# Eight first sums in turns by two k-tiles, the bias table in split products, and the last cross head's scores inside the output product

## The chip, the cores and the metric

One core of a Trainium2 chip runs the whole program. The metric is the device time in microseconds of one execution.

## The reference

One decoder layer on x (256 tokens, width 1024), all in float32:

```python
x = x + 0.5 * swiglu(rms_norm(x, g_ffn1), w_ffn1_gu, w_ffn1_down)   # width 2816
q/k/v = rms_norm(x, g_mix) @ w_in          # 12 dilated heads, 4 block-sparse heads
x = x + concat(rms_norm(oa), rms_norm(ob)) @ w_out    # both with a relative-position bias table
x = x + cross_attention(rms_norm(x, g_cross), rms_norm(mem, g_mem))  # 4 heads of 256, 256 memory tokens
x = x + 0.5 * swiglu(rms_norm(x, g_ffn2), w_ffn2_gu, w_ffn2_down)
out = rms_norm(x, g_final)

def swiglu(x, w_gu, w_down):
    g, u = split(x @ w_gu, 2)              # gate columns 0..2815, up columns 2816..5631
    return (silu(g) * u) @ w_down
```

The bias table is `rel_bias` (32 buckets x 16 heads), picked by a fixed one-hot matrix of buckets for 383 distances.

## The kernel before, in words

**Split products.** Weights and activations are kept as two parts in the type `float32r`, a high part (a rounded copy, written by ScalarE) and a low part (the rest, written by VectorE). A product is the sum of high x high, high x low and low x high. `wsplit` (L124) splits a weight tile, `split` (L314) an activation, with the norm's gain folded in. Activations are stored transposed, a k-tile being 128 features x 256 tokens with the high part in columns 0 to 255 and the low part in 256 to 511 of one slot. Some products are therefore one of 512 columns (high weight against both parts) and one of 256 (low weight): `mmT_run` (L219). `mmT_wide` (L232) and `mm3` (L187) do three of 256 columns.

**Weights.** A load brings 512 KB (two k-tiles x 512 columns) into one of four `raw` tiles; after the two parts of the split a raw tile is free again. The split tiles `w` are eight. All weight loads go through the SP queue. In `gate_up` (L415) each chunk takes 512 gate columns and 512 up columns (four blocks of 128 each); `each` (L262) goes block by block through all eight k-tiles of a chunk, in runs of two k-tiles.

**Order.** `start` (L754) is written out by hand for all engines (`manual_schedule()`): each engine does what the text gives it, in that order. From `gate_up` on only TensorE's order is as written, the other engines being ordered by a scheduler. Small steps are put into TensorE's stream by an estimated clock: `tick` adds the estimated time of each product, `later(delay, f)` runs f when that clock has gone on by delay, and `until` runs the waiting steps at once when a result is needed.

**The start.** x arrives in three loads and is turned by TensorE (`prepare`, L773, transposes at L779), copied to `X` and split. `prepare(j)` serves k-tiles 2j and 2j + 1 and, in the kernel before, also splits gate weight tile j. After WARM products on an identity matrix (L770, L796) come the gate sums: for each k-tile twelve products (L798), four blocks in four banks of the accumulator memory, with `prepare` of the next pair after every second k-tile. The up weights are then split, and the up sums follow (two blocks k-tile by k-tile at L811, two blocks one after the other at L816). The norm of x is applied afterwards: `token_squares` (L333) sums squares on ScalarE, `st.given` (L386) makes the root and a diagonal on GpSimd and VectorE, and `_rows` (L379) spreads it to all partitions as R by TensorE (L382). `turn_gains` (L74) transposes the other gains.

**The bias table.** `bias_table` (L88) loads a table of logarithms, the one-hot rows and `rel_bias`; `bias_rows` (L96) multiplies the last two in plain float32 (L98), adds, and sends the rows through device memory to the tables F that the attention adds to its scores. It is a hook after the second chunk of the first `gate_up`.

**Cross attention.** `cross_qp` (L678) makes the query blocks (L717), splits each, and puts `scores` of a head (L682: twelve products, then a softmax over both token halves) and its `turn` (L705: four transposes and a split) into the stream by `later`. `cross_o` (L729) multiplies the turned probabilities with V; `addT` (L466) does the output product with a written order of steps (L860), a step being (k, blocks) for k-tiles k and k + 1.

## Time and profile before

| | us |
|---|---|
| median of 3 runs (lowest, highest) | 605.53 (605.5, 606.17) |
| the profiled execution | 605.74 |
| its span | 604.0 |

The profile is of one execution. The span runs from the first to the last instruction; the rest of the time lies around it. Engines are TensorE (PE, its weight loads PEld), VectorE (DVE), ScalarE (ACT), GpSimd (POOL) and the queue SP. TensorE is busy 595.4 us of the span, VectorE 428.5, ScalarE 347.7. A row's duration on TensorE covers an instruction's own pipeline, so that neighbours overlap; the distance between starts is what an instruction costs.

### The profile page before, as it was taken

Reading aid. Unit: us, or ns where it says so; the run is one execution under the profiler, and the core shown is the slowest. Engines: PE = TensorE matmul, PEld = TensorE weight load, DVE = VectorE, ACT = ScalarE, POOL = GpSimd, SP = SyncE. Lnnn points to the kernel's source line nnn. Section 1 sums busy time; section 2 is a strip of 40 time slices with the busy share of each in tenths; the row PEclk is TensorE's granted clock in tenths of the full one; section 3 lists DMA queues with packets and bytes.
Section 4 is the critical chain, followed back from the end, with each engine's and each line's share of the span. In section 5 each row is a group of like instructions: output and inputs, shape, how many; then the busy total and the mean of one; then the engine's idle time right before and its main releaser. Section 6 shows DMA issues by size and latency. Waiting matters only on the chain.

```text
span 604.0 us, 9469 instructions
## 1 busy us (share of the span) xinstructions
PE 595.4 (99%) x3516; PEld 519.3 (86%) x3516; DVE 428.5 (71%) x716; ACT 347.7 (58%) x604; POOL 51.8 (9%) x83
## 2 busy tenths in 40 slices
PE   9999999999999999999999999999999999999995
PEld 8988888888899888888888899888888888888884
DVE  4788766887565876766897787869877877874412
ACT  6756446655554677656675565657755656653302
POOL 0000110000010102113300120003100000000000
PEclk9999999999999999999999999999999999999999
DMA  7867998677467636454446645444565565565401
GB/s 237 282 206 229 211 246 252 196 227 245 171 221 231 210 106 210 142 173 140 141 121 218 195 143 162 140 140 130 158 230 181 169 217 171 189 231 196 152 0 69
DMA packets 58989, 110.02 MB, mean 182 GB/s; under 512 B 3760, under 2 KB 14608, under 8 KB 58944
## 3 DMA queue, kind: packets, MB, share of 16 engines
q1 hardware_dynamic: 57664, 105.49, 54.1%
q0 software_dynamic: 832, 2.88, 2.8%
q10 hardware_dynamic: 448, 1.05, 0.5%
q8 instruction: 27, 0.44, 0.3%
q14 instruction: 18, 0.15, 0.1%
HBM read 107.58 MB, written 1.84 MB: 181 GB/s over the span
## 4 chain that ended last, share of the span: by engine, by line
PE 96%; issue 1%; DVE 1%; ACT 1%; POOL 0%; POOLq 0%; ACTq 0%
PE bank L224 43%; PE bank L228 22%; PE bank L188 7%; PE bank L189 7%; PE bank L190 7%; PE bank L238 5%; PE bank L518 1%; PE bank L575 1%; PE bank L558 1%; DVE w L126 0%; PE bank L770 0%; PE bank L382 0%; PE bank L779 0%; PE bank L873 0%; PE bank L604 0%
## 5 line engine op out<-in xcount | busy, mean ns | idle before, releaser
L224 PE MATMUL bank<-slot,w 128*128 128x512 f32 x1130 | 353.4, 396 | 0.0
L126 DVE TENSOR_TENSOR w<-raw,w 128x1024 fp32r<-128x1024 f32 (+1 forms) x197 | 237.3, 1219 | 84.5 <-ACT w L125 83.7
L125 ACT ACTIVATE w<-raw 128x1024 fp32r<-128x1024 f32 (+1 forms) x197 | 202.4, 1051 | 86.3 <-PE bank L190 43.4
L228 PEld LDWEIGHTS bank<-slot,w 128*128 128x128 f32 x1130 | 209.8, 188 | 48.7 <-issue 1.0
L228 PE MATMUL bank<-slot,w 128*128 128x256 f32 x1130 | 222.5, 279 | 0.0
L224 PEld LDWEIGHTS bank<-slot,w 128*128 128x128 f32 x1130 | 173.8, 189 | 2.5 <-issue 0.6
L188 PE MATMUL bank<-w,slot 128*128 128x512 f32 x152 | 60.0, 395 | 0.0
L190 PE MATMUL bank<-w,slot 128*128 128x512 f32 x152 | 59.3, 390 | 0.0
L189 PE MATMUL bank<-w,slot 128*128 128x512 f32 x152 | 59.2, 390 | 0.0
L277 ACT ACTIVATE hv<-bank 128x256 f32<-128x256 f32 x108 | 39.8, 375 | 33.7 <-PE bank L228 33.0
L320 ACT ACTIVATE slot<-u 128x512 fp32r<-128x512 f32 x22 | 13.8, 628 | 36.0 <-DVE u L434 36.0
L190 PEld LDWEIGHTS bank<-w,slot 128*128 128x128 f32 x152 | 28.5, 188 | 6.1
L188 PEld LDWEIGHTS bank<-w,slot 128*128 128x128 f32 x152 | 28.5, 188 | 6.0 <-issue 0.3
L189 PEld LDWEIGHTS bank<-w,slot 128*128 128x128 f32 x152 | 28.6, 188 | 5.5
L238 PE MATMUL bank<-slot,w 128*128 128x256 f32 x240 | 31.8, 290 | 0.0
L238 PEld LDWEIGHTS bank<-slot,w 128*128 128x128 f32 x240 | 30.1, 195 | 0.5 <-DVE slot L324 0.2
L355 POOL TENSOR_TENSOR ssq<-ssq,sq 128x256 f32<-128x256 f32 x22 | 20.5, 933 | 78.5 <-ACT sq L350 78.4
L429 ACT ACTIVATE g<-g 128x512 f32<-128x512 f32 x22 | 13.8, 631 | 20.1 <-DVE g L292 20.1
L324 DVE SCALAR_TENSOR_TENSOR slot<-X,gT,slot 128x256 fp32r<-128x256 f32 x30 | 19.4, 659 | 6.9 <-ACT slot L323 6.9
L321 DVE TENSOR_TENSOR slot<-u,slot 128x512 fp32r<-128x512 f32 x22 | 15.2, 691 | 10.7 <-ACT slot L320 10.5
L278 DVE TENSOR_TENSOR g<-bank,hv 128x256 f32<-128x256 f32 x40 | 16.5, 420 | 8.5 <-ACT hv L277 8.5
L323 ACT ACTIVATE slot<-X,gT 128x256 fp32r<-128x256 f32 x30 | 14.8, 506 | 13.0 <-DVE X L303 13.0
(128 smaller groups left out, 488.4 us busy)
## 6 DMA issues: line engine op xcount, KB each, us to landing
raw<-in_w_ffn_gu_dram SPq DMA_DIRECT2D x88, 512.0 KB, 4.6
raw<-in_w_ffn_down_dram SPq DMA_DIRECT2D x44, 512.0 KB, 4.3
raw<-in_w_ckv_dram SPq DMA_DIRECT2D x16, 512.0 KB, 5.5
raw<-in_w_in_dram SPq DMA_DIRECT2D x12, 512.0 KB, 3.7
raw<-in_w_in_dram SPq DMA_DIRECT2D x24, 256.0 KB, 4.0
raw<-in_w_out_dram SPq DMA_DIRECT2D x8, 512.0 KB, 4.5
raw<-in_w_cq_dram SPq DMA_DIRECT2D x8, 512.0 KB, 4.8
raw<-in_w_co_dram SPq DMA_DIRECT2D x8, 512.0 KB, 3.7
```

The source lines that it names most:

```text
L125: nc.scalar.activation(w[:, 0, a:b], raw[:, a:b], AF.Copy)
L126: nc.vector.tensor_tensor(w[:, 1, a:b], raw[:, a:b], w[:, 0, a:b].bitcast(F32), OP.subtract)
L188: nc.tensor.matmul(ps, ah, bh, start=start, stop=False)
L189: nc.tensor.matmul(ps, al, bh, start=False, stop=False)
L190: nc.tensor.matmul(ps, ah, bl, start=False, stop=stop)
L224: nc.tensor.matmul(ps, w[:, 0, o + blk * P:o + (blk + 1) * P], both(xs, k), start=k == first, stop=False)
L228: nc.tensor.matmul(ps[:, :256], w[:, 1, o + blk * P:o + (blk + 1) * P], both(xs, k)[:, :256], start=False, stop=k == last)
L238: nc.tensor.matmul(ps, w[:, wp_, o + blk * P:o + (blk + 1) * P], a, start=start and i == 0, stop=stop and i == 2)
L277: nc.scalar.activation(t, ps[:, 256:], AF.Copy)
L278: nc.vector.tensor_tensor(out, ps[:, :256], t, OP.add)
L324: nc.vector.scalar_tensor_tensor(l, src, g, h.bitcast(F32), OP.mult, OP.subtract)
L355: (eng or nc.gpsimd).tensor_tensor(new, self.ss, sq, OP.add)
```

## The change

In `start`, gate and up tiles are loaded, split and used in turns: for each pair of k-tiles 24 gate products (`products(j, pg0, ...)`) and 24 up products (`products(j, pu0, ...)`). A gate block and its up block share a bank, gate in columns 0 to 255 and up in 256 to 511; only the gate's first product carries the start flag. `prepare` no longer splits weights; `fetch` loads a raw tile. The first tile's first high half is written half by ScalarE and half by VectorE, and there are two products fewer in the second warm-up (an identity product is two instructions). R and the gains come with other delays.

In the bias table, `rel_bias` is split into two parts and the one-hot rows are copied to the split type, so that L98 becomes two products of 384 columns. Both are loaded into a raw tile.

In the cross attention, head 3's `scores` and `turn` are no longer put in by `later`; they are steps of the output product's order.

```diff
@@ -76,7 +76,6 @@
         nc.tensor.transpose(gps[:, :48], grow, ident[:48, :48])
         nc.vector.tensor_copy(gT, gps[:, :48])
 
-    rbt = const.tile([32, 16], F32, name="rbt")
     F = []
     X = [const.tile([P, 256], F32, name=f"X{k}") for k in range(KT)]
 
@@ -87,15 +86,22 @@
 
     def bias_table():
         lnt = work.tile([16, NB], F32, tag="g1", name="lnt", bufs=3)
-        oht = work.tile([32, NB], F32, tag="g1", name="oht", bufs=3)
         nc.sync.dma_start(lnt, lnc)
-        nc.sync.dma_start(oht, onehot)
-        nc.sync.dma_start(rbt, rel_bias)
-        later(4.0, bias_rows, lnt, oht)
-
-    def bias_rows(lnt, oht):
+        raw = rawp.tile([P, 1024], F32, tag="raw", name="raw")
+        nc.vector.memset(raw[:32, NB:384], 0.0)
+        nc.sync.dma_start(raw[:32, :NB], onehot)
+        nc.sync.dma_start(raw[:32, 512:528], rel_bias)
+        ohr = work.tile([32, 384], F32R, tag="pt", name="ohr", bufs=4)
+        rbs = small.tile([32, 2, 16], F32R, tag="rbs", name="rbs", bufs=1)
+        nc.scalar.activation(ohr, raw[:32, 0:384], AF.Copy)
+        nc.scalar.activation(rbs[:, 0], raw[:32, 512:528], AF.Copy)
+        nc.vector.tensor_tensor(rbs[:, 1], raw[:32, 512:528], rbs[:, 0].bitcast(F32), OP.subtract)
+        later(8.0, bias_rows, lnt, ohr, rbs)
+
+    def bias_rows(lnt, ohr, rbs):
         ps = bank()
-        nc.tensor.matmul(ps[:16, :NB], rbt, oht, start=True, stop=True)
+        for i in range(2):
+            nc.tensor.matmul(ps[:16, :384], rbs[:, i], ohr, start=i == 0, stop=i == 1)
         rb = work.tile([16, 384], F32, tag="u1", name="rb")
         nc.vector.tensor_add(rb[:, :NB], ps[:16, :NB], lnt)
         nc.vector.memset(rb[:, NB:], 0.0)
@@ -236,7 +242,7 @@
         for i, (wp_, a) in enumerate(((0, h), (0, l), (1, h))):
             for blk, ps in enumerate(pieces):
                 nc.tensor.matmul(ps, w[:, wp_, o + blk * P:o + (blk + 1) * P], a,
-                                 start=start and i == 0, stop=stop and i == 2)
+                                 start=start and i == 0, stop=stop and i == 2, skip_group_check=True)
                 tick(0.11)
 
     def projT(wk, xs, nblk, spread=False, whole=0, abreast=False):
@@ -700,7 +706,8 @@
                 nc.vector.reciprocal(rl, l)
                 nc.vector.tensor_scalar(pt, pt, rl, None, OP.mult)
                 pts[h][tb] = pt
-            later(5.0, turn, h)
+            if h < 3:
+                later(5.0, turn, h)
 
         def turn(h):
             tp = bank()
@@ -722,9 +729,9 @@
                     halves(t, ps)
                     ps = t
                 split(Q[-1], blk % 2, 1, ps)
-                if blk % 2:
+                if blk % 2 and (c, blk) != (1, 3):
                     later(3.0 + 3.0 * (blk // 2) * (c == 0), scores, c * 2 + blk // 2)
-        return PT
+        return PT, lambda: scores(3), lambda: turn(3)
 
     def cross_o(V, PT, OT, h):
         until(lambda: PT[h] is not None)
@@ -743,23 +750,25 @@
 
     st = Stats()
     xs = [slot() for _ in range(4)]
-    raws = [rawp.tile([P, 1024], F32, tag="raw", name="raw") for _ in range(4)]
-    ws = [wp.tile([P, 2, 1024], F32R, tag="w", name="w") for _ in range(4)]
-    first = [(ws[k // 2], (k % 2) * 512) for k in range(KT)]
-    pg0 = [bank()[:, :256] for _ in range(4)]
-
-    def load_w0(i):
-        nc.sync.dma_start(raws[i].rearrange("p (a n) -> p a n", n=512), cols(w_gu1, i * 2, 2, 0, 512))
+    gate, up = [], []
+    b0 = [bank() for _ in range(4)]
+    pg0, pu0 = [b[:, :256] for b in b0], [b[:, 256:] for b in b0]
+
+    def fetch(wk, c0):
+
+        raw = rawp.tile([P, 1024], F32, tag="raw", name="raw")
+        nc.sync.dma_start(raw.rearrange("p (a n) -> p a n", n=512), cols(w_gu1, len(wk), 2, c0, 512))
+        w = wp.tile([P, 2, 1024], F32R, tag="w", name="w")
+        wk += [(w, 0), (w, 512)]
+        return w, raw
 
     def start():
         load_x(0, 256)
         nc.scalar.dma_start(grow[0:8], g_ffn1.rearrange("l (k p) -> (l k) p", p=P))
-        load_w0(0)
+        g0, u0 = fetch(gate, 0), fetch(up, FF)
         load_x(256, 256)
-        load_w0(1)
+        g1, u1 = fetch(gate, 0), fetch(up, FF)
         load_x(512, 512)
-        load_w0(2)
-        load_w0(3)
         load_gains()
         make_identity(nc, ident)
         nc.vector.memset(ones, 1.0)
@@ -770,55 +779,71 @@
             nc.tensor.matmul(gps[:, :P], ident, ident, start=True, stop=True)
         nc.tensor.transpose(gps[:, :8], grow[0:8], ident[:8, :8])
         nc.vector.tensor_copy(gT1, gps[:, :8])
-        def prepare(j):
+        def turned(j):
             banks = [bank(), bank()] if j == 0 else [bank()] * 2
             xp = [banks[i][:, i * 256:i * 256 + 256] for i in range(2)]
             for i in range(2):
                 for tb in range(2):
                     o = tb * 512 + ((j * 2 + i) % 4) * P
                     nc.tensor.transpose(xp[i][:, tb * P:(tb + 1) * P], x0[j // 2][:, o:o + P], ident)
-            if j > 0:
-                wsplit(ws[j], raws[j], 0, 1024)
-                for i in range(2):
-                    nc.scalar.activation(X[j * 2 + i], xp[i], AF.Copy)
+            return xp
+
+        def prepare(j):
+            xp = turned(j)
             for i in range(2):
-                split(xs[j], i, 1, X[j * 2 + i] if j else xp[i], gain("ffn1", j * 2 + i))
-                if j == 0:
-                    wsplit(ws[j], raws[j], i * 512, i * 512 + 512)
-            if j == 0:
-                for i in range(2):
-                    nc.scalar.activation(X[i], xp[i], AF.Copy)
+                nc.scalar.activation(X[j * 2 + i], xp[i], AF.Copy)
+            for i in range(2):
+                split(xs[j], i, 1, X[j * 2 + i], gain("ffn1", j * 2 + i))
+
+        def products(j, pieces, wk, first):
+            for k in (j * 2, j * 2 + 1):
+                mmT_wide(pieces, wk, xs, k, first and k == 0, k == KT - 1)
 
         xss = [small.tile([P, 2], F32, tag=f"xss{hf}", name="xss", bufs=1) for hf in range(2)]
 
-        prepare(0)
-        for i in range(WARM - 1):
+        xp = turned(0)
+        split(xs[0], 0, 1, xp[0], gain("ffn1", 0))
+        w, raw = g0
+        nc.scalar.activation(w[:, 0, 0:256], raw[:, 0:256], AF.Copy)
+        nc.vector.tensor_copy(w[:, 0, 256:512], raw[:, 256:512])
+        nc.vector.tensor_tensor(w[:, 1, 0:512], raw[:, 0:512], w[:, 0, 0:512].bitcast(F32), OP.subtract)
+        split(xs[0], 1, 1, xp[1], gain("ffn1", 1))
+        wsplit(w, raw, 512, 1024)
+        wsplit(*u0, 0, 1024)
+        for i in range(2):
+            nc.scalar.activation(X[i], xp[i], AF.Copy)
+        for i in range(WARM - 2):
             nc.tensor.matmul(gps[:, :P], ident, ident, start=True, stop=True)
-        for k in range(KT):
-            mmT_wide(pg0, first, xs, k, k == 0, k == KT - 1)
-            if k % 2 == 0 and k < KT - 2:
-                prepare(k // 2 + 1)
-                if k == 2:
-                    token_squares(x0[0], xss[0])
-            if k == 5:
-                up.extend(colchunk(w_gu1, FF, 512))
-                token_squares(x0[1], xss[1])
-                nc.vector.tensor_tensor(xss[0], xss[0], xss[1], OP.add)
-                st.given(xss[0], 7.0)
-                later(4.0, turn_gains)
-        pu = [bank()[:, :256] for _ in range(2)]
-        for k in range(KT):
-            mmT_wide(pu, up, xs, k, k == 0, k == KT - 1)
-        b = bank()
-        for blk in range(2, 4):
-            pu.append(b[:, (blk - 2) * 256:(blk - 1) * 256])
-            for k in range(KT):
-                mmT(pu[-1], up, xs, k, blk, k == 0, k == KT - 1)
-        return pu
-
-    up = []
+        products(0, pg0, gate, True)
+        prepare(1)
+        wsplit(*g1, 0, 512)
+        wsplit(*g1, 512, 1024)
+        g2 = fetch(gate, 0)
+        products(0, pu0, up, False)
+        wsplit(*u1, 0, 1024)
+        u2 = fetch(up, FF)
+        products(1, pg0, gate, False)
+        prepare(2)
+        products(1, pu0, up, False)
+        wsplit(*g2, 0, 1024)
+        g3 = fetch(gate, 0)
+        token_squares(x0[0], xss[0])
+        products(2, pg0, gate, False)
+        prepare(3)
+        wsplit(*u2, 0, 1024)
+        u3 = fetch(up, FF)
+        products(2, pu0, up, False)
+        wsplit(*g3, 0, 1024)
+        token_squares(x0[1], xss[1])
+        nc.vector.tensor_tensor(xss[0], xss[0], xss[1], OP.add)
+        st.given(xss[0], 5.8)
+        later(2.0, turn_gains)
+        products(3, pg0, gate, False)
+        wsplit(*u3, 0, 1024)
+        products(3, pu0, up, False)
+
     with tc.manual_schedule():
-        pu0 = start()
+        start()
     with tc.manual_schedule(engines={mybir.EngineType.PE}):
         hid = gate_up(w_gu1, xs, st, (None, bias_table), (pg0, pu0))
         xs, st, block = next_x("mix")
@@ -851,14 +876,14 @@
         xs, st, block = next_x("cross")
         addT(w_out, ot, block)
         st.done(rows=False)
-        PT = cross_qp(xs, K, st)
+        PT, scores3, turn3 = cross_qp(xs, K, st)
         OT = []
         cross_o(V, PT, OT, 0)
         cross_o(V, PT, OT, 1)
         xs, st, block = next_x("ffn2")
         every = range(4)
-        addT(w_co, OT, block, ((0, every), (2, (0, 1)), lambda: cross_o(V, PT, OT, 2), (2, (2, 3)),
-                               lambda: cross_o(V, PT, OT, 3), (4, every), (6, every)))
+        addT(w_co, OT, block, ((0, (0, 1)), scores3, (0, (2, 3)), (2, (0, 1)), lambda: cross_o(V, PT, OT, 2), turn3,
+                               (2, (2, 3)), (4, (0,)), lambda: cross_o(V, PT, OT, 3), (4, (1, 2, 3)), (6, every)))
         st.done()
 
         hid = gate_up(w_gu2, xs, st, scale=0.5)
```

## Rows read from the trace of the kernel before

**Rows 1.** The page: the busy time of TensorE (us, share of the span, instructions), the granted clock in 40 slices, and the chain that ended last by engine.

```profile
PE 595.4 (99%) x3516; PEld 519.3 (86%) x3516; DVE 428.5 (71%) x716; ACT 347.7 (58%) x604; POOL 51.8 (9%) x83
...
PEclk9999999999999999999999999999999999999999
...
PE 96%; issue 1%; DVE 1%; ACT 1%; POOL 0%; POOLq 0%; ACTq 0%
```

**Rows 2.** The chain of waits in order of time, first 35 us: start us, us, what. L779 are the transposes of x, L796 and L770 the warm-up, L238 the products of `mmT_wide`.

```profile
1.35 2.50 PE bank L770 x10
...
4.05 1.04 PE bank L779 x4
5.09 1.71 PE bank L796 x8
...
8.75 0.44 PE bank L779 x4
9.19 3.06 PE bank L238 x24
...
12.69 2.88 PE bank L238 x24
...
16.01 6.26 PE bank L238 x49
...
22.46 3.44 PE bank L238 x27
```

**Rows 3.** The timeline of the first 40 us, all engines, around the first product: start us, us, engine, line, operation, out<-in, [idle before <-releaser].

```profile
5.62 0.63 ACT L125 ACTIVATE w<-raw 128x512 fp32r<-128x512 f32 x1 [0.44 <-DMA raw<-in_w_ffn_gu_dram]
...
6.45 2.30 PE L238 MATMUL bank<-slot,w 128*128 128x256 f32 x12
...
7.03 0.76 ACT L790 ACTIVATE X<-bank 128x256 f32<-128x256 f32 x2
```

**Rows 4.** The same timeline, around `prepare(2)`.

```profile
12.09 0.60 PE L779 MATMUL bank<-ident,slot 128*128 128x128 f32 x4
...
12.45 3.13 PE L238 MATMUL bank<-slot,w 128*128 128x256 f32 x24
...
12.73 0.66 ACT L783 ACTIVATE X<-bank 128x256 f32<-128x256 f32 x2 [0.69 <-PE bank L779]
...
14.07 0.63 ACT L337 ACTIVATE junk<-slot 128x512 bf16<-128x512 f32 x1
```

**Rows 5.** Timelines of the SP queue, ScalarE and VectorE from 10.9 to 31 us, in order of start. Of SP a row is an issue (or several merged).

```profile
10.97 0.32 SPq L93 DMA_DIRECT2D rbt<-in_rel_bias_dram  x1
...
12.48 26.43 SPq L118 DMA_DIRECT2D raw<-in_w_ffn_gu_dram  x13
...
22.04 1.06 ACT L125 ACTIVATE w<-raw 128x1024 fp32r<-128x1024 f32 x1 [1.51 <-DMA raw<-in_w_ffn_gu_dram]
...
23.00 0.61 ACT L337 ACTIVATE junk<-slot 128x512 bf16<-128x512 f32 x1
...
24.38 0.37 SPq L118 DMA_DIRECT2D raw<-in_w_ffn_gu_dram  x1
...
28.67 1.42 DVE L292 TENSOR_TENSOR g<-bank,R 128x256 f32<-128x256 f32 x4
...
29.28 1.06 ACT L125 ACTIVATE w<-raw 128x1024 fp32r<-128x1024 f32 x1 [0.99 <-DMA raw<-in_w_ffn_gu_dram]
...
30.66 1.22 DVE L126 TENSOR_TENSOR w<-raw,w 128x1024 fp32r<-128x1024 f32 x1
```

**Rows 6.** The chain of waits in order of time around the bias table's product (L98).

```profile
60.08 0.74 PE bank L98 x2
60.82 0.43 PE bank L224
61.25 0.23 PE bank L228 x2
61.49 0.47 PE bank L224 x2
```

**Rows 7.** Timelines of TensorE and VectorE around the scores of cross head 3, in order of start: L188 to L190 are the products of `mm3`, L321 on VectorE low halves (`slot<-hq` of a query block, `slot<-bank` of an output tile or of turned probabilities), L224 at 386.27 the first output product, L701 the last step of a softmax.

```profile
383.00 0.69 DVE L321 TENSOR_TENSOR slot<-bank,slot 128x512 fp32r<-128x512 f32 x1
...
383.67 0.28 PE L188 MATMUL bank<-slot 128*128 128x256 f32 x1
...
384.27 0.38 PE L188 MATMUL bank<-slot 128*128 128x256 f32 x1
...
384.74 0.42 DVE L321 TENSOR_TENSOR slot<-hq,slot 128x256 fp32r<-128x256 f32 x1
...
385.21 0.39 PE L189 MATMUL bank<-slot 128*128 128x256 f32 x1 [0.56 <-DVE slot L321]
...
386.27 0.63 PE L224 MATMUL bank<-slot,w 128*128 128x512 f32 x2
...
389.36 0.35 DVE L701 TENSOR_SCALAR cpt<-cpt,crl 128x256 f32<-128x256 f32 x1
```

**Rows 8.** Stretches of the end (from:to us, length), busy time and instructions of each engine, then PEclk (granted clock as a share of full), DMA share, GB/s.

```profile
597.60:601.70 4.10, 0.00 (x0) 0.00 (x0) 0.91 (x2) 1.39 (x3) 0.55 (x1) 1.00 0.24 90
...
601.90:604.00 2.10, 0.00 (x0) 0.00 (x0) 0.00 (x0) 0.00 (x0) 0.00 (x0) 0.50 0.12 41
```

## The prediction

> **What bounds the kernel now.** I read the page first: TensorE is busy 99% of the span, at the full granted clock in every slice, and the chain that ended last is 96% TensorE [rows 1]. The reader is to see that nothing off TensorE counts by itself; the time is the list of TensorE's instructions plus the few places where it stands still. So I next read the chain in order of time and looked for those places.
>
> At the start [rows 2] the chain is TensorE alone from 1.35 us. A group of 24 products of 256 columns takes 2.88 us where nothing waits, 0.120 us each. The groups of 24, 49 and 27 that took 3.06, 6.26 and 3.44 us therefore hold 0.18 + 0.38 + 0.20 = 0.76 us beyond that, of which I put 0.2 on the small transposes that cut into the stream: some **0.55 us of waits** is all that these groups have to give. In the bias table the two passes of L98 take 0.74 us and the product behind them 0.43 in place of 0.23 [rows 6]. In the cross attention the twelve score products of head 3 take 383.67 to 386.27, 2.60 us, against 12 x 0.120 = 1.44 us: TensorE waits first for ScalarE's high half of the last query block, then for VectorE's low half [rows 7], 1.16 us.
>
> The reference for the sum is the profiled execution, 605.74 us with a span of 604.0; the median of the runs shown is 605.53, 0.21 less. About 0.2% (1.2 us) is what a measurement of this kernel tells from no change.
>
> **First products.** The first weight tile's high half is now written half by ScalarE and half by VectorE. Before, ScalarE's 512 columns ran from 5.62 for 0.63 us and TensorE began at 6.45 [rows 3]; 256 columns take about 0.38 (the X copies' size [rows 3]), so the tile is ready 0.25 us earlier, and two fewer warm-up instructions (1.71 us for eight, 0.21 each [rows 2]) let TensorE be there. TensorE is at its lower clock level at that time (four transposes 1.04 us at 4.05, 0.44 us at 8.75 [rows 2]), so of the 0.25 I take 0.1 to 0.15. Using each x tile for gate and up halves the speed at which x and its splits are wanted, so the 0.55 us of waits should go; the diagonal for R is asked for only after all 192 products, so a wait for it can't cut in either. The order keeps as many products and transposes as before. Together **-0.7 us** (0 to -0.9; 0 if new small waits take their places, since the low half of g2 is ready about when it is wanted).
>
> **A wait that the new order makes.** All engines follow the written order in `start`. Third up pair, in the diff: `products(2, pg0)`, `prepare(3)`, `wsplit(*u2)`, `products(2, pu0)`. On ScalarE u2's split thus stands behind prepare(3), whose X copies wait for transposes that TensorE makes only after the gate products, while the very next products want u2. For the other pairs the split stands ahead of the next transposes, or a whole up group of 2.88 us lies between; here nothing does. Its length comes from prepare(2) of before, where ScalarE also waited for the transposes [rows 4]: transposes at 12.09, first X copy at 12.73, two copies and two gain splits, the next ScalarE instruction at 14.07, 1.98 us after. Then 1.06 us for u2's high half [rows 5], and 0.1 to 0.2 from ScalarE's end to a product (6.25 to 6.45 with the warm-up still ahead [rows 3]): 3.2 us after the transposes began. TensorE itself is free 0.36 us after (12.09 to 12.45 [rows 4]). Stall: **2.8 us**. The low half on VectorE ends 1.22 us after the high [rows 5], and the third group of four products wants it 8 x 0.12 = 0.96 us after the first: another 0.2 to 0.3. Behind the waiting X copies stand on ScalarE both gain splits, u2, g3, and the squares for R; all of them slide by as much, but g3 is wanted 2.9 us after u2 and follows 0.95 us behind it. I take **+3.0 us** (2.7 to 3.3). No work covers it: TensorE has nothing else in its order.
>
> Is the written order really ScalarE's? At 22.04 ScalarE stood 1.51 us for a load with the token squares behind it [rows 5], whose input the transposes of 12.09 had already read [rows 4]. That is the order as written, kept where it hurts.
>
> **The second chunk's gate weights.** Four raw tiles serve all loads. The raw tile of u3 is freed only when its low half is done. That instruction now stands on VectorE behind the copy of the gains (`turn_gains`), which waits for TensorE in the middle of the last gate group, some 2.3 us into it. Counted from the third transposes (T): TensorE resumes at T+3.2, ends the up group at T+6.3, gains turned at T+8.6, copied at T+9.1, u3's low half at T+10.4, last product and R at T+13.0. If the fourth gate tile of the second chunk takes u3's raw tile, it is loaded and its split begins 4.9 us after the issue (24.38 to 29.28 in the row of before [rows 5]): T+15.3, high half T+16.4, low T+17.6. The first block of the second chunk wants its last two k-tiles three runs of 0.70 us [rows 6] after T+13.0, T+15.1. That is a wait of 1.3 to 2.0 us, and 2.9 if the eight sums, now all read after R (0.36 us each [rows 5]), go ahead on VectorE. If another raw tile comes free earlier it is zero: loads of a later block can slip in front of `start`'s, as the bias load did at 10.97 ahead of the up loads [rows 5], so the first two splits may do so as well. I take **+0.9** (0 to 2.9), nearer to zero because of that row.
>
> **Bias table.** The two passes of 383 columns become two products of 384 in the split type. Nothing in the trace has 32 rows in that type; the nearest is L224, 512 columns in 0.23 us [rows 6], so 384 cost 0.175 and the pair 0.35 in place of 0.74. The cost at the edges (0.2 behind) I leave. **-0.4 us** (0 if the price per column stays, as the number of passes does, which also excludes a loss here; -0.6 if the edge goes too). The load of the table leaves the SP queue at 10.97 and comes, with the one-hot rows, through a raw tile: one of four is away for a load and a ScalarE copy, some 5 us, and SP's weight loads queue behind it. Eight split tiles, each worth four runs of 0.70 us (0.47 + 0.23 [rows 6]) to TensorE, cover that, and the product is planned 4 us later; without that cover one tile's 2.8 us would show. The table's result is first used in the attention, a whole half-step later. Zero.
>
> **Cross head 3.** Its twelve products move behind two runs of the output product (2 x 0.70 = 1.39 us), from 383.67 to 385.06; the fourth wants the last low half at 385.42, and VectorE had it at 385.16 [rows 7]. The first runs want the first output tile, low half done at 383.69 [rows 7]. So the 1.16 us go, up to 0.1. Late next is the softmax: before, its last step ended 389.71, 3.44 us after the scores [rows 7]; now it starts at 386.5 and its turn stands at 390.7, 0.75 us later than needed. Behind the turn, the first block of k-tiles 4 and 5 wants the third output tile 1.8 us after its product, against 0.6 + 0.7 us of splits with one weight split of 1.2 us possibly between. **-1.0 us** (-0.3 to -1.2). No DMA is issued by what moves.
>
> **Sum.** -0.7 + 3.0 + 0.9 - 0.4 - 1.0 = **+1.8 us**: 607.5 for the profiled execution, 607.3 for the median. With all ends: -0.9 + 2.7 + 0 - 0.6 - 1.2 = 0.0 to 0 + 3.3 + 2.9 + 0 - 0.3 = +5.9.
>
> **Rivals.**
> *The wait for u2 is not there (faster).* If u2's split reaches ScalarE ahead of the third prepare, TensorE runs on; the second chunk's loads then hurt by 0.3 at most: -0.7 + 0.3 - 0.4 - 1.0 = -1.8, **603.7**. For it: the early bias load on SP shows that the queues aren't wholly as written. Against it: that load belongs to no ordered block, u2's split does, and ScalarE kept its order in every row of [rows 4, 5]. It decides if the split moves up by 2 us. Chance 0.15.
> *Paid back (no change).* The stall is there, but raw tiles come free in time and bias and cross give their full ends: -0.8 + 3.0 + 0 - 0.5 - 1.1 = +0.6, **606.1**. Chance 0.25.
> *The clock falls in the stall (slower yet).* The granted clock stood at 1.00 until 601.7 and was 0.50 afterwards, the lower of the two levels; TensorE had done nothing since 597.6 [rows 8]. A stop of 2.8 us in which it issues nothing could do this amid the start. At the lower level it worked from 1.35 us into the products that begin at 6.45 [rows 3], and no longer at 8.75 [rows 2], 5 to 7.4 us at half speed; half of as long a stretch again is about 3 us: +1.8 + 3 = +4.8, **610.3**. Against it: there TensorE had stopped for good, here it goes on. Chance 0.08.
> The Trainium skill, "TensorE: Matmul & The Clock Gate", section "Why this matters for your kernels", warns of idle gaps between bursts of matmuls, after which the clock is at its lower rate; by that rule the time would be this rival's.
> The forecast itself has 0.52.
>
> **Numbers.** 607.3 us; the range 604.0 to 609.8 takes in nearly all of the forecast's own ends and the second rival, half of the first, and leaves the clock's case out. Faster by over 0.2%: 0.15 and the forecast's low end, 0.17. Same: 0.25. Slower: 0.58.
>
> **What would show it.** In the profile after: TensorE idle for 2.5 to 3 us near 23 to 26 us, released by ScalarE's split of w, with the transposes just ahead; ScalarE idle 2.5 us before those X copies; a first L224 at 35 to 36 us where it was 33.2, and a wait within 3 us behind it; L98's successors 0.35 us for two; no wait in head 3's scores. It is wrong if the 24 products behind the third transposes follow at once, or if the time falls below 605.

## The result, and the profile after

After: **612.65 us** median (612.12 to 613.49, 4 runs); before: 605.51 (605.14 to 606.17, 4 runs); ratio 1.0117 [1.0103, 1.013]. The change costs 7.1 us where 1.8 were forecast, outside the range. The profiled execution of after is 612.12 us with a span of 610.3, 6.3 longer than the span of before.

The page of after: busy time of TensorE and the others, granted clock, chain that ended last.

```profile
PE 597.0 (98%) x3514; PEld 520.6 (85%) x3514; DVE 429.1 (70%) x720; ACT 347.3 (57%) x607; POOL 52.0 (9%) x83
...
PEclk9899998999999999999999999999999999999998
...
PE 86%; DMA 6%; DVE 4%; issue 2%; ACT 2%; POOL 0%; POOLq 0%; ACTq 0%; SPq 0%; DVEq 0%
```

Against [rows 1] TensorE is busy 1.6 us longer, the clock has two new dents (slices 2 and 7, near 25 and 100 us), and the chain, 96% TensorE before, runs through DMA for 6% of the span. Something waits for loads now.

**The first stop**, timeline of TensorE from 18 to 37 us, then ScalarE's (start us, us, engine, line, operation, out<-in, [idle before <-releaser]). L788 are the transposes of x (L779 before), L244 is `mmT_wide` (L238), L230 and L234 are the two products of `mmT_run` (L224, L228 before), L131 and L132 the two halves of a split (L125, L126).

```profile
21.46 0.60 PE L788 MATMUL bank<-ident,slot 128*128 128x128 f32 x4
24.55 7.21 PE L244 MATMUL bank<-slot,w 128*128 128x256 f32 x43 [2.48 <-ACT w L131]
...
35.81 0.71 PE L230 MATMUL bank<-slot,w 128*128 128x512 f32 x2
```

```profile
22.10 0.66 ACT L794 ACTIVATE X<-bank 128x256 f32<-128x256 f32 x2 [2.75 <-PE bank L788]
...
23.44 2.00 ACT L131 ACTIVATE w<-raw 128x1024 fp32r<-128x1024 f32 x2
```

This is the forecast wait, with its two marks: the four transposes just ahead, ScalarE idle 2.75 us before its X copies. The rows of the second prepare of before [rows 4] had TensorE go on 0.36 us after the transposes; here it is 3.09. The second chunk starts at 35.81, 2.6 us later than before. Stretches of the same kernel (from:to us, length, busy time and instructions of each engine, then PEclk) show what followed both stops:

```profile
26.20:29.60 3.40, 3.40 (x18) 3.40 (x18) 2.43 (x6) 2.48 (x5) 0.72 (x1) 0.50 0.72 217
29.60:33.00 3.40, 3.40 (x28) 3.21 (x28) 1.23 (x3) 2.00 (x2) 0.00 (x0) 1.00 0.73 220
...
97.90:101.20 3.30, 2.96 (x10) 2.57 (x11) 2.90 (x6) 0.91 (x2) 0.00 (x0) 0.50 0.90 315
```

After each stop, when TensorE is already at work again, the granted clock is 0.50, the lower level (1.2 GHz), for some 3.4 us: 18 products in 3.4 us where the next 3.4 hold 28.

**The second stop** was not forecast. Timeline of TensorE, then the chain of waits in order of time (start us, us, what):

```profile
96.98 0.73 PE L230 MATMUL bank<-slot,w 128*128 128x512 f32 x2 [2.45 <-ACT w L131]
98.24 0.80 PE L234 MATMUL bank<-slot,w 128*128 128x256 f32 x2 [0.53 <-DVE w L132]
```

```profile
69.25 11.11 DMA raw<-in_w_ffn_gu_dram
...
80.38 1.07 ACT w L131
...
81.47 1.23 DVE w L132
...
82.73 13.12 DMA raw<-in_w_ffn_gu_dram
...
95.88 1.06 ACT w L131
```

Read it upwards: TensorE waits at 94.5 us for the last up tile of the fourth chunk; that tile's load took 13.12 us and could go out only when the low half of the tile before it in the same raw tile was done (82.70); and that tile's load had taken 11.11 us. Two slow loads in series use up all the slack that the split tiles hold. What is in their way, DMA traffic by queue in 72 to 76 us and in 84 to 88 us (packets, MB, share of 16 engines):

```profile
q0 software_dynamic: 87, 0.40, 97.2%
q1 hardware_dynamic: 6, 0.01, 0.8%
...
q0 software_dynamic: 239, 0.79, 98.6%
q1 hardware_dynamic: 23, 0.03, 4.6%
```

q1 carries the weights. In both stretches a weight load of the chain is under way, and q0 takes the engines: it is the bias table, its rows written 32 times and read back into F. The timeline of GpSimd's queue has it, in after and (second fence) in before:

```profile
68.40 0.84 POOL L109 DMA_DIRECT2D scr<-rb  x1 [40.43 <-DVE rb L106]
79.04 4.65 POOL L180 DMA_DIRECT2D F<-scr  x8 [9.80 <-DMA scr<-rb]
```

```profile
62.66 0.84 POOL L103 DMA_DIRECT2D scr<-rb  x1 [37.14 <-DVE rb L100]
73.71 4.63 POOL L174 DMA_DIRECT2D F<-scr  x8 [10.21 <-DMA scr<-rb]
```

The same transfers were there before, and a load of weights then also took long (the same tile's split began at 85.14 after 4.94 us of ScalarE waiting for its DMA), but it was issued at 72.99 us, not 82.73, and TensorE needed it near 92. Why the loads were late, ScalarE from 54 to 62 us of after (L96 and L97 the copies of the one-hot row and of the relative bias, L326 a hidden tile's high half):

```profile
54.75 0.20 ACT L97 ACTIVATE rbs<-raw 32x16 fp32r<-32x16 f32 x1
...
58.01 0.63 ACT L326 ACTIVATE slot<-u 128x512 fp32r<-128x512 f32 x1 [1.95 <-DVE raw L91]
58.55 0.51 ACT L96 ACTIVATE ohr<-raw 32x384 fp32r<-32x384 f32 x1
...
61.26 0.63 ACT L326 ACTIVATE slot<-u 128x512 fp32r<-128x512 f32 x1 [1.94 <-DVE u L440]
61.80 1.04 ACT L131 ACTIVATE w<-raw 128x1024 fp32r<-128x1024 f32 x1
```

The third chunk's up splits begin at 61.80; before, they began at 54.64. Ahead of them ScalarE now has both copies and two hidden tiles (L326), where before had one (53.84). The copies are short, 0.20 and 0.51 us, and L96 follows L326 without a wait. What costs is ScalarE's idling before the two hidden tiles, 1.95 and 1.94 us. The first of these rows names the memset L91, which ended at 57.98 us; the tile's own input, which VectorE makes at L440, ended at 57.97. The chain of waits in the same stretch runs through L440 both times and through neither copy (0.04 us of the bias difference, L98, stand between the first two rows):

```profile
57.38 0.60 DVE u L440
...
58.01 0.64 ACT slot L326
...
60.54 0.70 DVE u L440
...
61.80 1.05 ACT w L131
```

The tile that is split at 61.80 was asked for at 53.76 and had landed at 57.15.

**The small parts.** The bias product (timeline, first row) gives its place up after 0.44 us, in place of 0.74 [rows 6]. Head 3's twelve scores, now amid the output product, take 392.44 to 393.88, 1.44 us, the time of twelve products and no wait, where [rows 7] had 2.60.

```profile
66.54 0.52 PE L104 MATMUL bank<-ohr,rbs 32*16 32x384 f32 x2
66.98 0.39 PE L234 MATMUL bank<-slot,w 128*128 128x256 f32 x1
...
392.44 0.28 PE L194 MATMUL bank<-slot 128*128 128x256 f32 x1
...
393.88 0.63 PE L230 MATMUL bank<-slot,w 128*128 128x512 f32 x2
```

Matching L224 with L230 product by product, the shift against before is +2.60 us at 33 us, +2.40 behind the bias product, +7.29 from 101 us on, and +6.33 at the end, 0.96 having come back in head 3. So the second stop and what follows it cost 4.9 us: 2.6 for the stop, and 2.3 more because the products from 96.98 to 101.36 us take 4.38 us in place of 2.09. Of these some 0.8 are the wait for the tile's low half (98.24) and some 1.5 the lower clock.

### The profile page after: what moved, and what is told of

It is laid out like the page before. It is cut to its first block, busy times and chain, and to the rows that moved or that the text cites. A ratio compares the mean times of both kernels' runs of the same rounds, so it can differ in the third digit from the quotient of the medians.

```text
span 610.3 us, 9464 instructions
## 1 busy us (share of the span) xinstructions
PE 597.0 (98%) x3514; PEld 520.6 (85%) x3514; DVE 429.1 (70%) x720; ACT 347.3 (57%) x607; POOL 52.0 (9%) x83
## 3 DMA queue, kind: packets, MB, share of 16 engines
q1 hardware_dynamic: 57664, 105.49, 53.0%
q0 software_dynamic: 832, 2.88, 2.7%
## 4 chain that ended last, share of the span: by engine, by line
PE 86%; DMA 6%; DVE 4%; issue 2%; ACT 2%; POOL 0%; POOLq 0%; ACTq 0%; SPq 0%; DVEq 0%
PE bank L230 37%; PE bank L234 19%; PE bank L194 7%; PE bank L196 7%; PE bank L195 7%; DMA raw<-in_w_ffn_gu_dram 6%; PE bank L244 5%; DVE w L132 2%; PE bank L524 1%; PE bank L581 1%; PE bank L564 1%; ACT w L131 1%; DVE u L440 0%; PE bank L779 0%; PE bank L788 0%
## 5 line engine op out<-in xcount | busy, mean ns | idle before, releaser
L230 PE MATMUL bank<-slot,w 128*128 128x512 f32 x1130 | 354.3, 397 | 2.4 <-ACT w L131 2.4
L132 DVE TENSOR_TENSOR w<-raw,w 128x1024 fp32r<-128x1024 f32 (+1 forms) x197 | 236.5, 1216 | 82.7 <-ACT w L131 81.4
L131 ACT ACTIVATE w<-raw 128x1024 fp32r<-128x1024 f32 (+1 forms) x197 | 201.9, 1049 | 95.1 <-PE bank L196 42.8
L234 PEld LDWEIGHTS bank<-slot,w 128*128 128x128 f32 x1130 | 210.4, 189 | 50.1 <-issue 1.3
L234 PE MATMUL bank<-slot,w 128*128 128x256 f32 x1130 | 223.6, 280 | 0.5 <-DVE w L132 0.5
L230 PEld LDWEIGHTS bank<-slot,w 128*128 128x128 f32 x1130 | 174.4, 189 | 4.6 <-ACT w L131 2.6
L244 PE MATMUL bank<-slot,w 128*128 128x256 f32 x288 | 38.1, 293 | 2.5 <-ACT w L131 2.5
L244 PEld LDWEIGHTS bank<-slot,w 128*128 128x128 f32 x288 | 36.5, 199 | 3.2 <-ACT w L131 2.7
L326 ACT ACTIVATE slot<-u 128x512 fp32r<-128x512 f32 x22 | 13.8, 629 | 33.6 <-DVE u L440 31.7
L330 DVE SCALAR_TENSOR_TENSOR slot<-X,gT,slot 128x256 fp32r<-128x256 f32 x30 | 19.4, 659 | 14.2 <-ACT slot L329 14.2
L284 DVE TENSOR_TENSOR u<-bank,hv 128x256 f32<-128x256 f32 x40 | 16.7, 420 | 7.1 <-ACT hv L283 6.9
```

The lines of the kernel that those rows point to most:

```text
L131: nc.scalar.activation(w[:, 0, a:b], raw[:, a:b], AF.Copy)
L132: nc.vector.tensor_tensor(w[:, 1, a:b], raw[:, a:b], w[:, 0, a:b].bitcast(F32), OP.subtract)
L230: nc.tensor.matmul(ps, w[:, 0, o + blk * P:o + (blk + 1) * P], both(xs, k), start=k == first, stop=False)
L234: nc.tensor.matmul(ps[:, :256], w[:, 1, o + blk * P:o + (blk + 1) * P], both(xs, k)[:, :256], start=False, stop=k == last)
L244: nc.tensor.matmul(ps, w[:, wp_, o + blk * P:o + (blk + 1) * P], a, start=start and i == 0, stop=stop and i == 2, skip_group_check=True)
L284: nc.vector.tensor_tensor(out, ps[:, :256], t, OP.add)
```

## The experiments

All against the kernel before on the same chip (its medians: 605.75, 605.39 and 605.41 us in the three sets). A theory named by letters in the quoted texts is the one that the same text tells. The first set asks which part makes the stop at 94 us: the start, the bias part, both together, or the wait for u2.

**One part alone (three runs, and two together).** The edits are the hunks of the change, applied to the kernel before.

```
e1: cross_qp hands back scores(3), turn(3); addT(w_co, ...) calls them   (nothing else)
e2: fetch, turned, prepare, products and the new order in start          (nothing else)
e3: bias_table through a raw tile, two fp32r products, later(8.0, ...)   (nothing else)
e9: e1 and e3
```

> The kernel before with the cross part alone. All theories: 0.8 to 1.2 us faster than before, no wait in the scores of head 3; if the part is worth nothing by itself, within 0.3 us.

604.91 us (604.53 to 605.25, 10 runs), ratio 0.9986 [0.9977, 0.9996]: -0.84.

> The kernel before with the start part alone. The first product of the second chunk (33.2 us before) at about 35.8 us, a stop of 2.8 us near 22 us and a stretch at the lower clock behind it. Theory S (the weight loads that the start makes late are what starves TensorE at 94 us): the stop near 94 us is there too, 6 to 8 us slower in all. Theory B (the bias table's new place and raw tile starve it): no stop near 94 us, 2.3 to 3 us slower. Theory SB (it takes both): also 2.3 to 3 us.

608.61 us (608.42 to 610.55, 4 runs), ratio 1.0054 [1.0036, 1.0071]: +2.86. The profiled execution, 610.55 us, is the slowest of the four. No stop at 94 us. Another small wait shows, TensorE ahead of the bias product (its one-hot row, issued at 58.94, lands at 62.84), and in the profiled execution the lower clock comes after that wait and not after the first:

```profile
62.94 0.80 PE L98 MATMUL bank<-oht,rbt 32*16 32x383 f32 x2 [1.29 <-issue]
```

```profile
26.00:29.50 3.50, 3.45 (x30) 3.33 (x28) 2.52 (x7) 2.92 (x6) 0.72 (x1) 1.00 0.57 172
...
64.80:68.00 3.20, 3.20 (x12) 2.81 (x11) 3.17 (x7) 0.90 (x2) 0.84 (x1) 0.50 0.87 277
```

> The kernel before with the bias table's part alone. Theory S: 0.2 to 0.4 us faster, no stop. Theory B: a stop of several us near 91 us, 3 to 5 us slower. Theory SB: within 0.5 us of before, the weight tiles of the fourth chunk's up half ready later than before but in time.

605.15 us (604.81 to 605.66, 10 runs), ratio 0.9989 [0.9979, 0.9998]: -0.60. No stop at 94 us. The same copies stand on ScalarE, but only one hidden tile ahead of the third chunk's up splits:

```profile
53.73 0.63 ACT L326 ACTIVATE slot<-u 128x512 fp32r<-128x512 f32 x1 [1.94 <-DVE u L440]
...
54.53 2.00 ACT L131 ACTIVATE w<-raw 128x1024 fp32r<-128x1024 f32 x2
```

> The kernel before with the change's cross-attention and bias parts, its start as it was. If the parts add up where the start is not changed, the time is 605.4 less 0.8 and 0.6, 603.8 to 604.4 us, with no wait over 0.3 us between 80 and 100 us; if the bias part, with its raw tile, already costs the weight loads something that the cross part does not hide, 604.8 us or more.

604.19 us (603.78 to 605.14, 11 runs), ratio 0.9981 [0.9973, 0.999]: -1.2; the two add up within the noise.

The parts alone sum to +2.86 - 0.84 - 0.60 = +1.4, near the forecast's +1.8; the whole is +7.1. Some 5.7 us belong to none of them: the start and the bias part meet. That leaves theory SB: S wanted a stop in e2, B one in e3.

**The third up tile's split first (e4).**

```
+        wsplit(*u2, 0, 1024)
         products(2, pg0, gate, False)
         prepare(3)
-        wsplit(*u2, 0, 1024)
```

> The whole change, with the split of the third up tile put ahead of the third gate products on ScalarE and VectorE. The stop near 22 us and the lower clock behind it go: the second chunk starts at about 32 us in place of 35.8. Theory S: the stop at 94 us goes as well or shrinks below 1 us, 2 us faster than before. Theory B: it stays at 3 us or more, the whole 1 to 3 us slower than before. Theory SB: it shrinks by about half.

608.21 us (606.13 to 609.21, 8 runs), ratio 1.004 [1.0028, 1.0053]. The stop at 22 us is gone, and so is the one at 94 (one hidden tile stands ahead of the third chunk's up splits, which begin at 58.05), where theory SB had it halved; but a third comes, in the first block of the second chunk. Timelines of TensorE and of VectorE:

```profile
37.98 0.59 PE L234 MATMUL bank<-slot,w 128*128 128x256 f32 x2 [2.64 <-DVE w L132]
```

```profile
33.45 1.42 DVE L298 TENSOR_TENSOR g<-bank,R 128x256 f32<-128x256 f32 x4
...
36.71 1.22 DVE L132 TENSOR_TENSOR w<-raw,w 128x1024 fp32r<-128x1024 f32 x1
```

It is the prediction's wait for the second chunk's gate weights near its upper end: the low half of the fourth gate tile stands on VectorE behind the readings of the eight sums.

**Raw tile, delay or transfers (e5 to e7).** The chain names a slow load, but not why it met the table's transfers.

```
e5  -  raw = rawp.tile([P, 1024], F32, tag="raw", name="raw")
    +  oht = work.tile([32, 384], F32, tag="g1", name="oht", bufs=3)
    +  rb0 = small.tile([32, 16], F32, tag="rb0", name="rb0", bufs=1)
       (memset, loads and copies from these)
e6  -  later(8.0, bias_rows, lnt, ohr, rbs)
    +  later(4.0, bias_rows, lnt, ohr, rbs)
e7  -  nc.gpsimd.dma_start(scr, rb.unsqueeze(1).broadcast_to([16, 32, 384]))
    +  nc.gpsimd.dma_start(scr[:, 0], rb)
    -  later(5.0 * (i * 4 + a), nc.gpsimd.dma_start, f[32 * a:32 * a + 32], src)
    +  nc.gpsimd.memset(f, 0.0)
```

> The changed kernel, but the one-hot row and the relative bias are read into tiles of their own (as the one-hot row was before), so that the bias table takes none of the eight tiles into which weights are loaded. Theory R (the raw tile): the table holds a weight tile from about 46 to 59 us, every later weight load comes one tile later, and that is what makes the fourth up tile of the fourth chunk late at 94 us; then the first product of that chunk's late tile waits under 0.5 us, the load issued at 82.7 us goes out some us earlier, and the time is 607 to 609 us. Theory T (the table's own transfers): the loads of F and the spread rows go out at the same place as before this edit, the weight loads of 72 to 94 us crawl beside them, the stop at 94 us stays at 2 us or more and the time is 611.5 to 613.5 us.

607.57 us (606.59 to 607.92, 6 runs), ratio 1.0031 [1.0019, 1.0044]. No wait at 94 us, though the transfers leave at the same time (68.12 and 78.48). (The "eight tiles" of the expectation are the four raw ones.) ScalarE, its line numbers one higher:

```profile
56.35 1.06 ACT L132 ACTIVATE w<-raw 128x1024 fp32r<-128x1024 f32 x1 [0.25 <-PE bank L235]
...
62.09 0.51 ACT L97 ACTIVATE ohr<-oht 32x384 fp32r<-32x384 f32 x1
...
88.82 1.06 ACT L132 ACTIVATE w<-raw 128x1024 fp32r<-128x1024 f32 x1 [4.20 <-DMA raw<-in_w_ffn_gu_dram]
```

The third chunk's up splits now begin at 56.35, the first two ahead of the hidden tile, and the one-hot copy goes behind all four. The last up tile of the fourth chunk is still slow to load, but it is split at 88.82 and not 95.88: early enough.

> The changed kernel with the bias table's product asked for 4 us after its copies, as before the change, in place of 8. Theory D (the delay alone): the spread rows leave at about 64 us and not 68, the loads of F end some 4 us earlier, the last up tile of the fourth chunk is in time (no wait over 0.5 us at 94 us) and the time is 607 to 609 us. Theory T (transfers meet late weight loads): the transfers come earlier, but the weight loads of the third and fourth chunks that they meet are late already, by the stall at the start, so that a wait of 1 to 3 us appears somewhere from 85 to 96 us and the time is 610 to 613 us. Theory R: no change, 612 us.

616.04 us (615.58 to 616.79, 4 runs), ratio 1.0176 [1.016, 1.0191]: worse than after, as theory T had the direction, and more than it had in size. Asked for 4 us earlier, the rows left only 2.1 us earlier (66.27) and met the fourth chunk's gate loads; TensorE idles 1.1 to 1.6 us near 84, 97 and 99 us and the lower clock comes twice. That the delay alone makes the stop is excluded.

> The changed kernel without the bias table's large transfers: its rows are written once and not 32 times, and the tiles F are filled with zeros by GpSimd in place of the eight loads, so the self-attention's bias is left out of the output. Everything ahead of it (the raw tile, the copies, the two products) stays. Theory T: the weight loads of 72 to 94 us run at full rate, no wait at 94 us and no fall of the clock there, 607 to 608.5 us (605.5 with the parts' own +3.1, -0.8 and -0.6). Theory R: the raw tile still makes the loads late, a wait of 1 us or more remains near 94 us, 610 to 613 us.

608.71 us (608.56 to 609.09, 4 runs), ratio 1.0054 [1.0039, 1.0069]. No wait at 94 us. The start itself is 1.7 us late, because the fill of F sits on GpSimd ahead of the identity that the warm-up needs (the warm-up begins at 3.06 and not 1.35); without this the run stands near 607.0, an estimate, close to the 606.8 that the parts add up to. ScalarE's splits of the third chunk were late here too (64.34), so that delay alone makes no stop. Issues between 69 and 90 us (out<-in, queue, operation xcount, KB each, median us to landing), in after and in this run:

```profile
raw<-in_w_ffn_gu_dram SPq DMA_DIRECT2D x7, 512.0 KB, 11.0
```

```profile
raw<-in_w_ffn_gu_dram SPq DMA_DIRECT2D x10, 512.0 KB, 4.6
```

Beside the table's transfers a weight load takes 11.0 us (the median), without them 4.6. In before, beside the same transfers, it takes 14.2 in this stretch: the transfers slow the loads there too, but the late tile was asked for 9.7 us earlier.

**The slot or the order (e11).** In e5 both the raw tile and ScalarE's order changed. Here the row stays in a raw tile and only its four small operations move.

```
-        nc.vector.memset(raw[:32, NB:384], 0.0)
+        nc.gpsimd.memset(raw[:32, NB:384], 0.0)
   (the two copies and the difference: nc.scalar / nc.vector -> nc.gpsimd, the same way)
```

> The changed kernel, its one-hot row still in a raw weight tile, but the memset, the two copies and the difference on GpSimd and not on VectorE and ScalarE. Theory O (order): what makes the weights late is that ScalarE's bias copies at 54.8 and 58.6 us, and VectorE's memset at 57.9 us that they wait for, stand ahead of the third chunk's up splits; on GpSimd they hold nobody, those splits begin at 56 to 57 us and not at 61.8, the wait at 94 us is under 0.5 us and the time is 607 to 608.5 us. Theory S (the slot): it is the raw tile being held from 51.7 to 58.6 us; the loads of the tiles behind it come as late as in the changed kernel, the wait at 94 us stays at 2 us or more and the time is 611 to 613 us.

607.63 us (606.59 to 609.35, 6 runs), ratio 1.0037 [1.0025, 1.005]; no wait at 94 us, one of 0.38 us at 105. The splits begin at 57.14. GpSimd holds the raw tile until 55.6 and nobody else. So the tile comes free earlier as well (in after at 59.1), but in after that did not bind: the load behind the split at 61.80 was in at 57.15, and the next pause of SP's weight loads, from 59.08 to 64.12, ended with that tile's low half (64.10). The order on ScalarE is what counted.

**Both mends (e8, e10).** e8 moves the splits of the third and fourth up tiles forward; e10 is e8 with the tiles of e5.

```
+        wsplit(*u2, 0, 1024)
+        u3 = fetch(up, FF)
         products(2, pg0, gate, False)
         prepare(3)
-        wsplit(*u2, 0, 1024)
-        u3 = fetch(up, FF)
         products(2, pu0, up, False)
         wsplit(*g3, 0, 1024)
+        wsplit(*u3, 0, 1024)
```

> The changed kernel with the third up tile's split ahead of the third gate products and of the fourth transposes, the fourth up tile fetched there and split ahead of the token squares' second half. The wait of 2.48 us for that tile at 22 us goes (the second chunk's products begin at 32 to 32.5 us, not 35.8), as in the run with the third up tile alone moved; new here is that VectorE's work after the first chunk stands otherwise. If a late lo half of the second chunk's fourth gate tile was what cost 2.8 us at 35 us in that run, as the theory of the evacuations has it, it is still late by 1 to 3 us and the time is 606 to 609 us; if it was late because of the up tile's split behind it, the stop is under 1 us and the time is 603 to 605 us. At 94 us no wait in either case.

609.84 us (607.52 to 610.58, 4 runs), ratio 1.0065 [1.0043, 1.0088]. No stop at 22 or 35 us, as the second of the two cases had it, but from 90.7 us one of 3.59, which neither had: in the chain two weight loads in series again, 10.79 us from 66.13 and 13.85 us from 79.29. With the start quicker the need comes 3 us earlier and ScalarE's order is the same as in after: two hidden tiles, at 54.89 and 58.14, ahead of the third chunk's up splits from 58.68. The second chunk begins at 31.97 us here, earlier than in the kernel before (33.22), so that a late start is not what this stop needs.

> The changed kernel with both mends: the third and fourth up tiles split (and the fourth fetched) early, as in the run with those two moved, and the one-hot row in a tile of its own, as in the run with that alone. By the theory (one wait at 22 us from the order of the splits, one at 94 us from the bias table's raw tile and its copies ahead of the weight splits) both waits go: 607.6 less the stall of 2.5 us, 603 to 605.5 us, with the granted clock full from 6 us to the end and no wait over 0.7 us. If the weight loads that run beside the table's transfers are late whatever holds the splits, a wait of 1 us or more stays near 85 to 94 us and the time is 606 to 609 us.

**603.78 us** (603.07 to 605.1, 11 runs), ratio 0.9974 [0.9965, 0.9983]: faster than both kernels, with no wait over 0.7 us. Its page's chain, and the row of TensorE that answers to 24.55 of after:

```profile
PE 98%; issue 1%; POOL 0%; DVE 0%; ACT 0%; POOLq 0%
```

```profile
21.76 5.57 PE L245 MATMUL bank<-slot,w 128*128 128x256 f32 x43
```

Ratios to before of the four combinations:

| | u2, u3 split as changed | split early |
|---|---|---|
| one-hot row in a raw tile | 1.0117 (after) | 1.0065 (e8) |
| in a tile of its own | 1.0031 (e5) | 0.9974 (e10) |

The tile is worth 0.86 to 0.91% (5.2 to 5.5 us), the order of the splits 0.52 to 0.57% (3.1 to 3.5 us); the two add up within their intervals, and they explain the loss.

**Which order it is.** Counted in the timelines, ScalarE has two hidden tiles ahead of the third chunk's up splits in after, e6, e7 and e8, one in before, e1, e3, e4 and e9, and none ahead of the first of them in e2, e5, e10 and e11. The late stop shows in those of the first group that have the table's transfers (after, e6 and e8) and in no other run; e3, e4 and e9 have the same copies on ScalarE. Why the scheduler gives ScalarE the order with two in those four kernels, no run shows.

## Why the prediction was wrong

| term | forecast | in the profile of after |
|---|---|---|
| first products | -0.7 | -1.6 |
| wait for u2 | +3.0 | +2.7 |
| lower clock behind it | rival, 0.08, 3 | +1.5 |
| second chunk's gate weights | +0.9 (0 to 2.9) | 0 |
| bias product | -0.4 | -0.2 |
| the table's raw tile and delay | 0 | +4.9, of which some 1.5 the lower clock |
| cross head 3 | -1.0 | -0.96 |
| sum | +1.8 | +6.3 |

**The step that failed** is the end of the part on the bias table: "Eight split tiles, each worth four runs of 0.70 us ... cover that ... Zero." It priced the raw tile as one load and one copy's delay, and took the split tiles as full cover at any time; the term measured +4.9 us. Two things stood in its place. With the bias operations among its work ScalarE has two hidden tiles ahead of the third chunk's up splits, and these begin at 61.80 us; on the old start the scheduler puts one there, and the same copies cost nothing (e3). And the table's own transfers, on GpSimd's queue and named nowhere in the prediction, slow the weight loads from 4.6 to 11 us or more just when the late loads are wanted. Taking away the order (e5, e11) or the transfers (e7) removes the stop; each is needed, neither is enough. The prediction weighed SP's queue and left GpSimd's out, although the page's list of DMA queues has its traffic.

**The wait for u2** came as worked out: place, length (2.76 us from the last transpose to the product), marks and first L230. e5 and e10 give the price with what follows it: 0.57%, 3.5 us.

**The clock's rival**, given 0.08, came true after both stops, at half its price. The cost is read from two rows with the same wait and the same 43 products, 7.21 us in after and, in the execution of e11 that kept its clock,

```profile
24.83 5.71 PE L244 MATMUL bank<-slot,w 128*128 128x256 f32 x43 [2.48 <-ACT w L131]
```

1.5 us. The Trainium skill, "TensorE: Matmul & The Clock Gate", section "Why this matters for your kernels", warns of long idle gaps between bursts of matmuls, after which the clock is at the lower rate. The gaps that it warns of are longer than the stops here, and in after the clock fell behind both (2.48 and 2.45 us), so by these rows the warning reaches too little; in e11 it did not fall after the same 2.48 us. The rival's own time, 610.3, is nearer the result than the forecast by the accident that its 3 us equal two falls.

**The first products** gained more than forecast, and part of it isn't the change's. Products of TensorE between 5.75 and 7.85 us, before and then after:

```profile
5.75:7.85 2.10, 2.10 (x11) 2.10 (x11) 1.57 (x3) 2.04 (x5) 0.00 (x0) 1.00 1.01 372
```

```profile
5.75:7.85 2.10, 2.10 (x19) 2.09 (x19) 1.84 (x4) 2.04 (x5) 0.00 (x0) 1.00 1.02 337
```

The clock column has 1.00 in both rows; the distance between starts tells more. In before instructions start 0.21 us apart until 7.88 us, in after only until 5.73, and 0.11 to 0.12 apart from there on. The eight more instructions are worth about 1 us, an estimate at 0.12 each, which leaves some -0.6 of the -1.6 for the change itself, about the size that was forecast. The rest is not the change's: e9, whose start is that of before, holds 18 in the same stretch, so that the moment at which the full rate comes differs from execution to execution. Between e9 and e10, both with an early rise, the start with its splits mended gives 1.17 us at the first L230 (32.56 to 31.39), and 0.41 in the medians.

**The second chunk's gate weights** cost nothing here, the end that was taken as the nearer one; e4 showed the other end, 2.64 us, where the stop ahead of it was gone.

**The cross part** was right: -0.96 in the trace, -0.84 alone, and no new wait for its turn.

## What to carry to other kernels

When a small table goes through the buffers and engines of the main stream, look at what its own transfers do to the stream's loads, not only at how long its tile is away. Where a scheduler orders an engine, a few short operations more can come with another order of the long ones: compare what stands ahead of the weight splits in the two timelines, not only the prices of the new operations. A wait named after a small instruction may belong to a neighbour that ended at the same moment; the chain of waits tells. Parts of a change that were priced one by one are to be timed together as well.

## What the runs showed of the hardware that was not expected

In two stretches of the table's transfers the weights get almost nothing: 6 packets to 87 in 4 us, and 23 to 239. The Trainium skill, "DMA: Bandwidth & Descriptors", section "Queues, rings and completion order", has each engine take turns between the queues that it has work for, packet by packet, a packet there being several descriptors. An estimate by that rule, if a turn takes as many of the profile's packets from either queue, with 1.8 KB to one of the weights (105.49 MB in 57664) and 3.5 KB to one of the table's (2.88 MB in 832), is a third of the bytes for the weights. In these stretches the trace does not agree: a load of the chain is under way throughout both, and q1 has 0.8% and 4.6% of the engines. What holds its packets back, the runs do not show.

The granted clock does not fall after every stop of the same length: after 2.48 us of idling it fell in the profiled executions of after, e5 and e7 and not in those of e2 and e11; after 1.29 us in e2 it fell. It came 0.3 us (e4) to 1.7 us (e2, e7) after TensorE had resumed, stayed for about 3.4 us (6.8 behind two waits in e6), and cost 1.5 us in the rows compared above. In e5 the one execution with a mean granted clock of 0.997 took 606.59 us, those with 0.994 and 0.995 from 607.32 to 607.92.
